# Attention scores: full-width weights of a head pair, 16 KB store runs, and an earlier start of the second unit's transposes

## Chip, cores and metric

One core of a Trainium2 chip. The metric is the device time of an execution in microseconds. PE is the profile's name for TensorE; an eviction is the copy of a finished tile of scores from PSUM into the store tile. Ratios are computed as the mean time of one kernel's fast runs over that of the other's of the same rounds, so a ratio is not quite the ratio of the medians quoted beside it.

## The reference

```python
batch, heads, seq, dim = 8, 8, 512, 64          # q and k, float32
def reference(q, k):
    scale = 1.0 / np.sqrt(q.shape[-1])
    return (np.einsum('bhqd,bhkd->bhqk', q, k) * scale).astype(np.float32)
```

Two inputs of 8.4 MB go in and 67.1 MB of scores come out.

## The kernel before

The work is cut into 4 units of two batches (16 heads, in 8 pairs). Inputs of a unit are loaded, cast to bf16 on GpSimd, and transposed on TensorE. Queries go into a zero-padded tile `qz`, so that one matmul over 128 rows serves the two heads of a pair. `take(ahead, n)` puts `n` steps of the next unit's transposes behind an eviction. A store tile has 32 KB per partition; three such buffers serve loads and stores together.

```python
RO = 16                                     # output rows per run
U = S // RO                                 # 32 runs per head
out_r = out.rearrange("(v b) (t h) (u i) k -> v (b t) (h u) (i k)", b=2, h=4, i=RO)
big_pool = ctx.enter_context(tc.tile_pool(name="big", bufs=3))
...
def matmul(v, t, i, x, dst):
    kT, qz = ts[v]
    pinned(nc.tensor.matmul(out=dst, lhsT=qz[:, i, 2 * t + x, :],        # 64 columns
                            rhs=kT[:, 2 * t + x].rearrange("d m s j -> d (m s j)"),
                            start=True, stop=True))

def scores(v, t):
    o = big_pool.tile([P, RO, S], f32, name="big")
    for i in range(0, RO, 2):
        ps = psum_pool.tile([P, 2, S], f32, name="ps")
        for w in range(2):
            for x in range(2):
                matmul(v, t, i + w, x, ps[half(x), w, :])
        evacuate(o[:, i:i + 2, :], ps)      # ScalarE and VectorE share these
        yield
    src = o.rearrange("p i k -> p (i k)")
    nc.sync.dma_start(out=out_r[v, t], in_=src)
...
for v in range(UNITS):
    ahead = transpose(v + 1, *cast[v + 1]) if v + 1 < UNITS else iter(())
    for t in range(TILES):
        for n, _ in enumerate(scores(v, t)):
            take(ahead, 1 + (n % 4 == 3) if v else 2 * (t > 0))
```

Of the kernel before, what the change touches and what calls it, by code (L numbers as in the profile page):

```python
# [1 line left out]

# [5 lines left out]


@with_exitstack  # L10
def kernel(
    ctx: ExitStack,
    tc: tile.TileContext,
    q: bass.AP,
    k: bass.AP,
    out: bass.AP,
):






    nc = tc.nc
    B, H, S, D = q.shape
    scale = 1.0 / (D ** 0.5)
    P = 128
    UNITS = B // 2
    N = H
    M = P // (2 * H)  # L30
    R = S // M
    J = R // 2
    RO = 16
    U = S // RO
    JJ = J // RO
    IW = 8 // JJ
    TILES = N // 2

    f32 = mybir.dt.float32
    bf16 = mybir.dt.bfloat16  # L40

    q_r = q.rearrange("(v b) g (m j) d -> v (b g m) (j d)", b=2, j=R)
    k_r = k.rearrange("(v b) g (m j) d -> v (b g m) (j d)", b=2, j=R)
    out_r = out.rearrange("(v b) (t h) (u i) k -> v (b t) (h u) (i k)", b=2, h=4, i=RO)

    consts = ctx.enter_context(tc.tile_pool(name="consts", bufs=1))

    big_pool = ctx.enter_context(tc.tile_pool(name="big", bufs=3))
    bf_pool = ctx.enter_context(tc.tile_pool(name="bf", bufs=6))
    t_pool = ctx.enter_context(tc.tile_pool(name="t", bufs=2))  # L50
    tpsum_pool = ctx.enter_context(tc.tile_pool(name="tpsum", bufs=2, space=bass.MemoryType.PSUM))
    psum_pool = ctx.enter_context(tc.tile_pool(name="psum", bufs=3, space=bass.MemoryType.PSUM))


    pinned = tc.keep_in_program_order

    n_evac = 0
    n_tp = 0

    def evacuate(dst, src):  # L60
        nonlocal n_evac

        if n_evac % 6 in (0, 2, 3):
            pinned(nc.scalar.mul(out=dst, in_=src, mul=scale))  # L64
        else:
            pinned(nc.vector.tensor_scalar(out=dst, in0=src, scalar1=scale, scalar2=None,  # L66
                                           op0=mybir.AluOpType.mult))
        n_evac += 1

    def half(h):  # L70
        return slice(h * D, (h + 1) * D)

    def load_and_cast(v):

        xf = big_pool.tile([P, 2, 2, J * D], f32, name="big")
        both = []
        for x, src in enumerate((k_r, q_r)):
            nc.sync.dma_start(out=xf[:, x], in_=src[v].rearrange("p (s c) -> p s c", s=2))
        for x in range(2):
            xb = bf_pool.tile([P, J, 2, D], bf16, name="xb")  # L80
            for s in range(2):
                pinned(nc.gpsimd.tensor_copy(out=xb[:, :, s, :],  # L82
                                             in_=xf[:, x, s].rearrange("p (j d) -> p j d", j=J)))
            both.append(xb)
        return both

    def rearrange(tp, pattern, dst):

        nonlocal n_tp
        copy = (nc.vector.tensor_copy, nc.scalar.copy)[n_tp % 2]  # L90
        n_tp += 1
        for s in range(2):
            src = tp[half(s)].rearrange(pattern, n=N, h=2)
            for h in range(2):
                pinned(copy(out=dst(s, h), in_=src[:, h]))  # L95
                yield

    def transpose(v, kb, qb):


        kT = t_pool.tile([P, N, M, 2, J], bf16, name="kT")
        qz = qzs[v % 2]
        ts[v] = (kT, qz)
        for j0 in range(0, J, 8):
            tp = tpsum_pool.tile([P, 8, P], bf16, name="tp")
            for j in range(8):
                pinned(nc.tensor.transpose(out=tp[:, j, :], identity=identity,  # L107
                                           in_=kb[:, j0 + j].rearrange("p s d -> p (s d)")))
            yield
            yield from rearrange(tp, "d j (n h m) -> d h n m j",  # L110
                                 lambda s, h: kT[half(h), :, :, s, j0:j0 + 8])
        for i0 in range(0, RO, IW):
            tp = tpsum_pool.tile([P, IW, JJ, P], bf16, name="tp")
            for i in range(IW):
                for jj in range(JJ):
                    pinned(nc.tensor.transpose(out=tp[:, i, jj, :], identity=identity,  # L116
                                               in_=qb[:, RO * jj + i0 + i].rearrange("p s d -> p (s d)")))
            yield
            yield from rearrange(tp, "d i jj (n h m) -> d h i n m jj",
                                 lambda s, h: qz[half(h), i0:i0 + IW, :, h * U:(h + 1) * U]  # L120
                                 .rearrange("d i n (m s jj) -> d s i n m jj", s=2, jj=JJ)[:, s])

    def matmul(v, t, i, x, dst):

        kT, qz = ts[v]
        pinned(nc.tensor.matmul(out=dst, lhsT=qz[:, i, 2 * t + x, :],  # L126
                                rhs=kT[:, 2 * t + x].rearrange("d m s j -> d (m s j)"),
                                start=True, stop=True))

    def scores(v, t):  # L130

        o = big_pool.tile([P, RO, S], f32, name="big")
        for i in range(0, RO, 2):
            ps = psum_pool.tile([P, 2, S], f32, name="ps")
            for w in range(2):
                for x in range(2):
                    matmul(v, t, i + w, x, ps[half(x), w, :])
            evacuate(o[:, i:i + 2, :], ps)
            yield
        src = o.rearrange("p i k -> p (i k)")  # L140
        nc.sync.dma_start(out=out_r[v, t], in_=src)  # L141

    def take(steps, count):
        for _ in range(count):
            next(steps, None)

    identity = consts.tile([P, P], dtype=bf16)
    make_identity(nc, identity)
    qzs = [consts.tile([P, RO, N, 2 * U], bf16, name=f"qz{n}") for n in range(2)]
    for qz in qzs:  # L150
        nc.vector.memset(qz, 0.0)  # L151
    cast = [load_and_cast(v) for v in range(UNITS)]

    ts = {}
    for _ in transpose(0, *cast[0]):
        pass
    for v in range(UNITS):
        ahead = transpose(v + 1, *cast[v + 1]) if v + 1 < UNITS else iter(())
        for t in range(TILES):

            for n, _ in enumerate(scores(v, t)):
                take(ahead, 1 + (n % 4 == 3) if v else 2 * (t > 0))
        for _ in ahead:
            pass


# [1 line left out]
_INS = ['q', 'k']  # L168
_OUTS = [((8, 8, 512, 512), 'float32')]


# [23 lines left out]
```

## Time and profile before

| | before |
|---|---|
| median of 4 runs | 203.72 us (203.69 to 203.80) |
| span of the profiled run | 202.1 us |
| score matmuls and weight loads | 512 + 512, weights of 64 columns |
| store packets | 2048 of 32 KB |
| instructions recorded | 1976 |

The lines that bound the kernel are shown in the prediction. Three more from the page: the score matmuls (busy time, mean ns of one, idle time before them), the queue that fetches instructions (packets, MB, share), and the time from a store's issue to its landing.

```profile
L126 PE MATMUL ps<-kT,qz 128*64 128x512 bf16 x512 | 85.0, 456 | 47.2 <-ACT big L64 36.6
...
q8 instruction: 6, 0.10, 0.2%
...
out_dram<-big SPq DMA_DIRECT2D x16, 4096.0 KB, 21.2
```

### The profile page before, as it was taken

Reading aid. Unit: us, or ns where it says so; the run is one execution under the profiler, and the core shown is the slowest. Engines: PE = TensorE matmul, PEld = TensorE weight load, DVE = VectorE, ACT = ScalarE, POOL = GpSimd, SP = SyncE. Lnnn points to the kernel's source line nnn. Section 1 sums busy time; section 2 is a strip of 40 time slices with the busy share of each in tenths; the row PEclk is TensorE's granted clock in tenths of the full one; section 3 lists DMA queues with packets and bytes.
Section 4 is the critical chain, followed back from the end, with each engine's and each line's share of the span. In section 5 each row is a group of like instructions: output and inputs, shape, how many; then the busy total and the mean of one; then the engine's idle time right before and its main releaser. Section 6 shows DMA issues by size and latency. Waiting matters only on the chain.

```text
span 202.1 us, 1976 instructions
## 1 busy us (share of the span) xinstructions
PE 107.7 (53%) x768; PEld 55.7 (28%) x768; DVE 126.4 (63%) x130; ACT 101.1 (50%) x129; POOL 30.5 (15%) x22
## 2 busy tenths in 40 slices
PE   0033488663784767765858685856765366710000
PEld 0033344332342333332423332322322133400000
DVE  6736677974987689997569797479457064530000
ACT  2016665793639586974857566746526241520000
POOL 1277777655000000000000000000000000000000
PEclk9999999998769999997878888888589957555555
DMA  6999999999999999999999999999999999999991
GB/s 214 428 444 415 435 441 422 418 412 428 454 438 417 441 417 428 438 448 435 422 415 425 448 435 448 415 418 428 435 448 441 415 428 438 441 428 441 415 415 58
DMA packets 3464, 84.00 MB, mean 416 GB/s; under 512 B 384, under 2 KB 384, under 8 KB 384
## 3 DMA queue, kind: packets, MB, share of 16 engines
q1 hardware_dynamic: 3456, 83.89, 97.2%
q8 instruction: 6, 0.10, 0.2%
q14 instruction: 2, 0.02, 0.0%
HBM read 16.78 MB, written 67.11 MB: 415 GB/s over the span
## 4 chain that ended last, share of the span: by engine, by line
DMA 33%; DVE 14%; PE 6%; ACT 2%; issue 1%; DVEq 0%; ACTq 0%; SPq 0%
DMA out_dram<-big 33%; DVE big L66 9%; PE ps L126 6%; DVE kT L95 3%; ACT big L64 2%; DVE qz L95 1%; ACT kT L95 1%; PE tp L107 0%; DVEq L66 0%; ACTq L64 0%; SPq L141 0%
## 5 line engine op out<-in xcount | busy, mean ns | idle before, releaser
L126 PE MATMUL ps<-kT,qz 128*64 128x512 bf16 x512 | 85.0, 456 | 47.2 <-ACT big L64 36.6
L66 DVE TENSOR_SCALAR big<-ps 128x1024 f32<-128x1024 f32 x64 | 76.2, 1221 | 38.9 <-DMA out_dram<-big 25.0
L64 ACT ACTIVATE big<-ps 128x1024 f32<-128x1024 f32 x64 | 63.9, 1023 | 56.9 <-DMA out_dram<-big 24.5
L126 PEld LDWEIGHTS <-qz 128*64 128x64 bf16 x512 | 35.6, 124 | 85.9 <-issue 75.7
L82 POOL CAST xb<-big 128x2048 bf16<-128x2048 f32 x16 | 29.8, 1893 | 17.1 <-DMA big<-in_k_dram 9.6
L95 DVE COPY kT<-tp 64x512 bf16<-64x512 bf16 x32 | 22.0, 687 | 7.3 <-PE tp L107 6.9
L95 ACT COPY kT<-tp 64x512 bf16<-64x512 bf16 x32 | 18.5, 578 | 15.2 <-PE tp L107 14.9
L95 DVE COPY qz<-tp 64x512 bf16<-64x512 bf16 x32 | 22.0, 688 | 3.9 <-PE tp L116 3.3
L95 ACT COPY qz<-tp 64x512 bf16<-64x512 bf16 x32 | 18.5, 578 | 4.0 <-PE tp L116 3.6
L107 PE MATMUL tp<-identity,xb 128*128 128x128 bf16 x128 | 12.0, 253 | 15.0 <-POOL xb L82 12.4
L116 PE MATMUL tp<-identity,xb 128*128 128x128 bf16 x128 | 13.3, 272 | 7.8 <-ACT qz L95 4.1
L107 PEld LDWEIGHTS <-xb 128*128 128x128 bf16 x128 | 9.5, 114 | 20.8 <-POOL xb L82 12.4
L116 PEld LDWEIGHTS <-xb 128*128 128x128 bf16 x128 | 10.6, 123 | 14.4 <-issue 14.1
L151 DVE MEMSET qz<- 128x4096 uint32 x2 | 6.9, 3472 | 2.5 <-PEq L179 1.7
L95 ACT ACT_TABLE_LOAD x1 | 1.3, 1283 | 0.7 <-PEq L179 0.7
masks.py:199 POOL TENSOR_SCALAR_AFFINE_SELECT identity<-identity 128x128 bf16<-128x128 bf16 x1 | 0.3, 292 | 0.1
masks.py:197 POOL MEMSET identity<- 128x128 bf16 x1 | 0.2, 204 | 0.3 <-POOLq L179 0.3
L179 POOL MEMSET const-float32-0.0<- 128x1 f32 x1 | 0.1, 98 | 0.2 <-issue 0.2
L179 POOL MEMSET const-bfloat16-1.0<- 128x1 bf16 x1 | 0.1, 101 | 0.0
L179 POOL MEMSET const-uint8-127<- 128x1 uint8 x1 | 0.1, 101 | 0.0
L179 POOL MEMSET const-float32-1.0<- 128x1 f32 x1 | 0.1, 98 | 0.0
## 6 DMA issues: line engine op xcount, KB each, us to landing
out_dram<-big SPq DMA_DIRECT2D x16, 4096.0 KB, 21.2
big<-in_k_dram SPq DMA_DIRECT2D x4, 2048.0 KB, 18.9
big<-in_q_dram SPq DMA_DIRECT2D x4, 2048.0 KB, 23.9
```

Of the source, the lines that this page charges most:

```text
L64: pinned(nc.scalar.mul(out=dst, in_=src, mul=scale))
L66: pinned(nc.vector.tensor_scalar(out=dst, in0=src, scalar1=scale, scalar2=None, op0=mybir.AluOpType.mult))
L82: pinned(nc.gpsimd.tensor_copy(out=xb[:, :, s, :], in_=xf[:, x, s].rearrange("p (j d) -> p j d", j=J)))
L95: pinned(copy(out=dst(s, h), in_=src[:, h]))
L107: pinned(nc.tensor.transpose(out=tp[:, j, :], identity=identity, in_=kb[:, j0 + j].rearrange("p s d -> p (s d)")))
L116: pinned(nc.tensor.transpose(out=tp[:, i, jj, :], identity=identity, in_=qb[:, RO * jj + i0 + i].rearrange("p s d -> p (s d)")))
L126: pinned(nc.tensor.matmul(out=dst, lhsT=qz[:, i, 2 * t + x, :], rhs=kT[:, 2 * t + x].rearrange("d m s j -> d (m s j)"), start=True, stop=T ...
L151: nc.vector.memset(qz, 0.0)
L179: nc = _bacc.Bacc("TRN2", target_bir_lowering=False, num_devices=1)
```

## The change

The intent: weights of the full 128 columns, so that half as many matmuls and weight loads do the same work. For that a partition holds 8 output rows (16 KB) of each of two pairs instead of 16 rows (32 KB) of one. The second unit's transposes begin already with the first store tile.

```diff
-    RO = 16
+    RO = 8
-    out_r = out.rearrange("(v b) (t h) (u i) k -> v (b t) (h u) (i k)", b=2, h=4, i=RO)
+    out_r = out.rearrange("(v b) (t x h) (u i) k -> v (b t) (h u) x (i k)", b=2, x=2, h=2, i=RO)
 ...
-        o = big_pool.tile([P, RO, S], f32, name="big")
-        for i in range(0, RO, 2):
-            ps = psum_pool.tile([P, 2, S], f32, name="ps")
-            for w in range(2):
-                for x in range(2):
-                    matmul(v, t, i + w, x, ps[half(x), w, :])
-            evacuate(o[:, i:i + 2, :], ps)
-            yield
-        src = o.rearrange("p i k -> p (i k)")
-        nc.sync.dma_start(out=out_r[v, t], in_=src)
+        o = big_pool.tile([P, 2, RO, S], f32, name="big")
+        for x in range(2):
+            n = 2 * t + x
+            for i in range(0, RO, 2):
+                ps = psum_pool.tile([P, 2, S], f32, name="ps")
+                for w in range(2):
+                    pinned(nc.tensor.matmul(out=ps[:, w, :], lhsT=qz[:, i + w, n, :],
+                                            rhs=kT[:, n].rearrange("d m s j -> d (m s j)"),
+                                            start=True, stop=True))
+                evacuate(o[:, x, i:i + 2, :], ps)
+                yield
+        nc.sync.dma_start(out=out_r[v, t], in_=o.rearrange("p x i k -> p x (i k)"))
 ...
-    qzs = [consts.tile([P, RO, N, 2 * U], bf16, name=f"qz{n}") for n in range(2)]
+    qzs = [consts.tile([P, RO, N, P], bf16, name=f"qz{n}") for n in range(2)]
 ...
-                take(ahead, 1 + (n % 4 == 3) if v else 2 * (t > 0))
+                take(ahead, 1 + (t > 0 if v == 0 else n % 4 == 3))
```

More of the change, by code (lines that the diff above doesn't have):

```diff
@@ L121, in transpose, with scores @@
                                  .rearrange("d i n (m s jj) -> d s i n m jj", s=2, jj=JJ)[:, s])
-    def matmul(v, t, i, x, dst):
+    def scores(v, t):
         kT, qz = ts[v]
-        pinned(nc.tensor.matmul(out=dst, lhsT=qz[:, i, 2 * t + x, :],
-                                rhs=kT[:, 2 * t + x].rearrange("d m s j -> d (m s j)"),
-                                start=True, stop=True))
-    def scores(v, t):
-        o = big_pool.tile([P, RO, S], f32, name="big")
-        for i in range(0, RO, 2):
-            ps = psum_pool.tile([P, 2, S], f32, name="ps")
-            for w in range(2):
-                for x in range(2):
-                    matmul(v, t, i + w, x, ps[half(x), w, :])
-            evacuate(o[:, i:i + 2, :], ps)
-            yield
-        src = o.rearrange("p i k -> p (i k)")
-        nc.sync.dma_start(out=out_r[v, t], in_=src)
+        o = big_pool.tile([P, 2, RO, S], f32, name="big")
[10 more added lines that the diff above has]
+        nc.sync.dma_start(out=out_r[v, t], in_=o.rearrange("p x i k -> p x (i k)"))
     def take(steps, count):
```

## The prediction

> **What bounds the kernel now.** I read the page from the top. No compute engine is near its limit; the DMA row of the slices is.
>
> ```profile
> span 202.1 us, 1976 instructions
> PE 107.7 (53%) x768; PEld 55.7 (28%) x768; DVE 126.4 (63%) x130; ACT 101.1 (50%) x129; POOL 30.5 (15%) x22
> DMA  6999999999999999999999999999999999999991
> DMA packets 3464, 84.00 MB, mean 416 GB/s; under 512 B 384, under 2 KB 384, under 8 KB 384
> q1 hardware_dynamic: 3456, 83.89, 97.2%
> ```
>
> The busiest compute engine, VectorE, works 63% of the span; the 16 DMA engines work 97.2% of it with one queue's packets, 196.4 us of 202.1 each. Then the stretches, to see where the missing 3% lies and at what rate each phase runs (columns: stretch, its length, the engines' busy times, clock, DMA share, GB/s):
>
> ```profile
> 2.00:4.00 2.00, 0.00 (x0) 0.00 (x0) 2.00 (x1) 0.01 (x1) 0.00 (x0) 1.00 0.73 238
> 5.00:38.00 33.00, 15.42 (x126) 10.51 (x128) 22.10 (x26) 14.31 (x22) 22.38 (x12) 1.00 1.01 430
> 45.00:195.00 150.00, 86.94 (x596) 42.27 (x595) 94.75 (x97) 78.58 (x98) 3.22 (x2) 0.80 1.00 432
> 197.00:199.00 2.00, 0.00 (x0) 0.00 (x0) 0.00 (x0) 0.00 (x0) 0.00 (x0) 0.50 0.31 131
> 199.00:201.00 2.00, 0.00 (x0) 0.00 (x0) 0.00 (x0) 0.00 (x0) 0.00 (x0) 0.50 0.04 16
> ```
>
> From 4 us to 195 us the transfers never pause: loads (5 to 38 us) at 430 GB/s, stores (45 to 195 us) at 432. What is not transfer is about 2 us of start and, at the end, some 6 us in which engines run out one after the other (share 0.31, then 0.04: one straggler) and the program closes. Last, the chain of waits, to see how much room the compute side has inside this:
>
> ```profile
> 120.15 22.27 DMA out_dram<-big
> ...
> 142.52 1.03 ACT big L64
> 143.55 0.04 issue
> 143.60 4.49 PE ps L126 x20
> 148.09 0.02 issue
> 148.11 1.24 DVE big L66
> ...
> 149.40 22.66 DMA out_dram<-big
> ```
>
> A 4 MB store waits for a free 32 KB-per-partition buffer, is filled in 149.40 - 142.42 = 7.0 us, and then takes 22.66 us to land. Its own bytes need 4.194 MB / 432 GB/s = 9.7 us; the other 13 us are queueing behind earlier stores and the landing itself. So the chain alternates fill and store, but the DMA is never empty meanwhile: with three buffers, when one lands, two stores are still due, about 19.4 us of transfer less some 2 us already moved, 17 us against a fill of 7 to 11 us (the store issues in the sync engine's timeline lie 7.4 to 12.9 us apart). The compute side has 6 us or more to spare per tile. **The bound is bytes over DMA rate, plus a cost per packet.**
>
> [...]in its DMA records a 4-byte completion packet takes 9 ns, a 16 KB packet (all 1024 of the loads) 611 ns at the median, a 32 KB packet (all 2048 of the stores) 1213 ns. Two of 611 make 1222, so again 9 ns for one packet more. [...]Before, a store's 32 runs of a head lie side by side and the four heads 1 MiB apart, at 432 GB/s; after, runs are 16 KB apart, with 1 MiB between heads and 2 MiB between the pairs. No run of before shows the new mix; the loads, with rows 16 KB apart, ran at 430. [...]The trace has weight-load gaps of 0.41 to 0.81 us around the transposes[...].
>
> **The change part by part.**
> *Weights.* 512 matmuls with 64 columns become 256 with 128, each still streaming 512 columns; 512 weight loads become 256. In the trace four half-width matmuls that serve one eviction span 0.62 us at full clock, and twenty span 4.49 us at the low clock (0.90 us per eviction): the halves already ran side by side. Two full-width ones should span the same 0.45 to 0.9 us. So half the PE instructions go, and little PE time. On the path that sets the end: 0. The other queue fetches instructions, six packets of 16 KB in the records; were they all for the 768 + 768 PE instructions, each would take 64 bytes (an estimate), and 512 fewer would save two fetches, about 0.6 us each on the DMA engine that serves them, which counts only if that is the straggler. Expected value, an estimate: -0.2 us.
> *Evictions.* 64 + 64 of 128x1024 elements as before, 1.22 us on VectorE and 1.02 on ScalarE. 0.
> *Transposes and copies.* As many tiles (8 per unit) and copies (32 of 512 elements). The destination's inner run of the query copies grows from 2 to 4 elements; copies with runs of 8 (kT) and of 2 (qz) take 687 and 688 ns, so run length is free. 0.
> *Store runs.* Every 32 KB store packet becomes two of 16 KB: 16 stores x 256 = 4096 instead of 2048. By the records 4096 x 611 - 2048 x 1213 = 18,400 ns, over 16 engines 1.15 us each. This lies on the bound, since the engines have no pause in which to hide it: +1.15 us. Nothing else about a store changes: 4 MB, 16 of them, three buffers.
> *Order in the first unit.* The second unit's transposes start with the first store tile: 8 steps there, 16 in the second and third, none in the fourth (before: 0, 16, 16, 8). They need the second unit's casts:
>
> ```profile
> 23.28 3.73 POOL L82 CAST xb<-big 128x2048 bf16<-128x2048 f32 x2 [1.17 <-DMA big<-in_q_dram]
> 28.91 1.23 DVE L66 TENSOR_SCALAR big<-ps 128x1024 f32<-128x1024 f32 x1
> 33.07 3.73 POOL L82 CAST xb<-big 128x2048 bf16<-128x2048 f32 x2 [1.17 <-DMA big<-in_q_dram]
> 35.05 22.20 SPq L141 DMA_DIRECT2D out_dram<-big  x3
> ```
>
> The second unit is cast at 27.0 us, before the first eviction at 28.9, so TensorE will not block. The 8 steps put four copies of 0.69 us on VectorE and two of 0.58 on ScalarE among the evictions: the first store issues at about 36.5 to 37.5 us instead of 35.05. The loads keep the DMA busy until 16.78 MB / 430 GB/s + 2.3 = 41.3 us, so 4 us remain. The second tile can't be filled before the third unit's casts end at 36.8 us, which is so before and after; it has until 51, and issued at 44.06. The third issued at 56.91, waiting for the last casts, and has until 60.7. The fourth comes some 2 us earlier. On the path: 0.
> Sum: 203.74 + 1.15 - 0.2 = 204.7 us. I shade it to 204.6, because the many half-size packets may even out the last microseconds a little.
>
> **The rivals.**
> *The larger strides slow the HBM writes.* [...]Against: [...]the loads ran at the same rate. If the rate lost 3%, stores of 155 us would add 4.7 us: 208.4.
> *The first store comes too late.* For: VectorE gets 2.75 us more work before it, and TensorE takes the transposes in order. Against: the 4 us of slack. If it were missed by 2 us, the DMA would idle 2 us: 206.7.
> *Less PE work makes it faster.* For: TensorE waits and weight loads stand in the chain (PE 6%). Against: a tile filled sooner only joins the queue sooner. Only the straggler could give time: the last engine ends at 200.8 us, the next at 198.9 in the records, so at most 1.9 us of gain, less the 1.15: about 203.
> *Packets stay 32 KB*, read as one run from SBUF: then nothing changes, 203.6.
>
> **Range and chances.** The packet term is worked from three medians that agree, so I trust it to a few tenths if packets do halve. The straggler may move by a microsecond either way without the change being its cause; the runs of before spread only 0.1 us. That gives 203.4 to 205.8. Two per cent is 4.1 us: faster by that would need more than the whole start and end tail that could be won, and I give it 1%. Slower by that needs the stride rival, 2%.
>
> **What would show it.** Right: 4096 store packets (5504 in the hardware queue), 16 KB medians near 611 ns, DMA share 1.0 from 4 to 195 us, store rate 430 instead of 432, 256 matmuls of full width with PE idle more, first store issued near 37 us, and the end about 1 us later. Wrong: a share below 0.97 in any stretch between 36 and 62 us (the order's cost), packets well over 611 ns (strides), or packets still of 32 KB. A straggler that ends much earlier or later than 200.8 us would make the size wrong with the mechanism right.

Passages that nothing in this case shows are cut from this text, and the cuts are marked: a rate that the transfers were compared with (that nothing was left to win inside them was not shown); a reason for a cost per packet, which the records then measure ("in its DMA records" means the trace's); a cause of the weight-load gaps; and reasons for and against the rival of the strides, which stands without a "For". 203.74 + 1.15 - 0.2 = 204.69, told as 204.7 and shaded to 204.6.

## The result

The changed kernel takes 203.02 us (202.95 to 203.29, 4 runs) against 203.72; the ratio is 0.9968, with a 95% interval of 0.995 to 0.9985. It became 0.3% faster where 0.4% slower was forecast, and it lies below the range, which began at 203.4.

The page of the changed kernel: its span, the engines, the DMA row, the packets, and the two queues.

```profile
span 201.3 us, 1456 instructions
PE 99.2 (49%) x503; PEld 48.3 (24%) x512; DVE 126.4 (63%) x130; ACT 100.7 (50%) x129; POOL 30.6 (15%) x22
DMA  6999999999999999999999999999999999999993
DMA packets 5510, 83.97 MB, mean 417 GB/s; under 512 B 384, under 2 KB 384, under 8 KB 384
q1 hardware_dynamic: 5504, 83.89, 98.1%
q8 instruction: 4, 0.07, 0.1%
L132 PE MATMUL ps<-kT,qz 128*128 128x512 bf16 x247 | 81.1, 450 | 55.1 <-ACT big L64 39.2
```

The store packets halved in size as foreseen (5504 in the hardware queue), TensorE's score matmuls are busy almost as long with half the instructions (81.1 us against 85.0), and the DMA row is just as full. The DMA's share rose from 97.2 to 98.1%: its engines do more work in a shorter span, so the gain lies in how the work ends. The stretches show it (the same columns as in the prediction):

```profile
5.00:38.00 33.00, 13.87 (x107) 10.14 (x109) 21.93 (x26) 15.37 (x24) 22.41 (x12) 1.00 1.01 430
45.00:195.00 150.00, 80.85 (x369) 35.95 (x374) 94.31 (x97) 77.73 (x97) 3.74 (x2) 0.80 1.01 430
...
197.00:199.00 2.00, 0.00 (x0) 0.00 (x0) 0.00 (x0) 0.00 (x0) 0.00 (x0) 0.50 0.50 213
199.00:201.00 2.00, 0.00 (x0) 0.00 (x0) 0.00 (x0) 0.00 (x0) 0.00 (x0) 0.50 0.04 16
```

Stores run at 430 GB/s instead of 432, as the prediction said. But from 197 to 199 us half of the engines' time is busy instead of 0.31: more engines end together, later than before, and the last one ends sooner.

The trace makes this exact. It has 16 completion signals for each transfer (384 for the 24 of either kernel), with their times, and at 60, 100, 150 and 190 us its packet records show 16 data packets in flight. I read the 16 signals as one from each of the 16 DMA engines; the trace doesn't say which engine is which. For each store, take the time of the median engine and how far behind it the last one is (all in us, from the profiled run):

| store | before: median | last behind | after: median | last behind |
|---|---|---|---|---|
| 1st | 52.31 | 1.70 | 52.14 | 2.51 |
| 6th | 100.92 | 1.60 | 100.79 | 2.44 |
| 8th | 120.38 | 2.11 | 120.34 | 2.38 |
| 10th | 139.85 | 2.56 | 139.78 | 2.34 |
| 12th | 159.23 | 2.93 | 159.29 | 2.29 |
| 14th | 178.60 | 3.29 | 178.76 | 2.22 |
| 16th | 197.95 | 3.28 | 198.40 | 2.03 |

The median engine ends 0.45 us later, the last one 197.95 + 3.28 - 198.40 - 2.03 = 0.80 us earlier, as the span does (202.1 to 201.3). Before, one engine fell behind steadily, from the 6th store on some 0.2 us per store, until the compute ended at 179 us; after that its lag stood still. The column of the changed kernel needs care: it falls, because it shows whichever engine is last. In that profile one engine was late from the start (2.51 us) and came closer, while the second-last fell behind, from 0.80 us at the 1st store to 2.21 at the 14th; at the end the two are 0.08 us apart. In the run called old order below, which has the same score instructions and packets, the last lag grows from 1.29 us at the 7th store to 2.17 at the 14th and ends at 2.00. So the lag at the first store varies from profile to profile (1.25 to 2.51 us), and the lag at the end repeats (2.03 and 2.00). In the packet records of before, the falling behind shows as one train of 32 KB packets that take mostly 1226 to 1293 ns instead of 1213, each beginning where the one before it ended, from 41.9 to 179 us; their excess sums to 3.9 us. (It is more than the growth in the table, since until the 5th store another engine seems to have been last, whose lag fell.) So there are two questions: does the lag come from the number of PE instructions, from the packet size, or from the order; and what do the packets themselves cost?

### The profile page after: what moved, and what is told of

Same layout as the page of the kernel before. It is cut to its first block, busy times and chain, and to the rows that moved or that the text cites. A ratio compares the mean times of both kernels' runs of the same rounds, so it can differ in the third digit from the quotient of the medians.

```text
span 201.3 us, 1456 instructions
## 1 busy us (share of the span) xinstructions
PE 99.2 (49%) x503; PEld 48.3 (24%) x512; DVE 126.4 (63%) x130; ACT 100.7 (50%) x129; POOL 30.6 (15%) x22
## 3 DMA queue, kind: packets, MB, share of 16 engines
q1 hardware_dynamic: 5504, 83.89, 98.1%
## 4 chain that ended last, share of the span: by engine, by line
DMA 63%; DVE 16%; PE 3%; POOL 3%; ACT 1%; POOLq 1%; issue 1%; SPq 0%; DVEq 0%; ACTq 0%
DMA out_dram<-big 43%; DMA big<-in_q_dram 20%; DVE big L66 12%; PE ps L132 3%; DVE qz L95 3%; POOL xb L82 3%; DVE kT L95 1%; ACT big L64 1%; POOLq L186 1%; SPq L78 0%; DVEq L66 0%; SPq L137 0%; ACTq L64 0%; POOLq L82 0%
## 5 line engine op out<-in xcount | busy, mean ns | idle before, releaser
L132 PE MATMUL ps<-kT,qz 128*128 128x512 bf16 x247 | 81.1, 450 | 55.1 <-ACT big L64 39.2
L132 PEld LDWEIGHTS <-qz 128*128 128x128 bf16 x256 | 27.5, 111 | 96.0 <-issue 83.2
L107 PE MATMUL tp<-identity,xb 128*128 128x128 bf16 x128 | 12.0, 254 | 16.5 <-POOL xb L82 12.5
L116 PE MATMUL tp<-identity,xb 128*128 128x128 bf16 x128 | 12.8, 265 | 6.0 <-DVE kT L95 3.5
L107 PEld LDWEIGHTS <-xb 128*128 128x128 bf16 x128 | 10.5, 116 | 20.8 <-POOL xb L82 12.8
L116 PEld LDWEIGHTS <-xb 128*128 128x128 bf16 x128 | 11.3, 122 | 10.9 <-issue 8.9
```

The costliest lines, as they stand in the source:

```text
L107: pinned(nc.tensor.transpose(out=tp[:, j, :], identity=identity, in_=kb[:, j0 + j].rearrange("p s d -> p (s d)")))
L116: pinned(nc.tensor.transpose(out=tp[:, i, jj, :], identity=identity, in_=qb[:, RO * jj + i0 + i].rearrange("p s d -> p (s d)")))
L132: pinned(nc.tensor.matmul(out=ps[:, w, :], lhsT=qz[:, i + w, n, :], rhs=kT[:, n].rearrange("d m s j -> d (m s j)"), start=True, stop=True))
```

## The experiments

Theory 1: each instruction, on whatever engine, costs one DMA engine a little, and that engine sets the end. Theory 2: smaller packets share the engines out more evenly. Theory 3: the new order of the first unit changes, by chance, how late the last engine is. The first three runs take the change apart.

**Split weights.** The changed kernel with 512 half-width matmuls again.

```diff
-    pinned(nc.tensor.matmul(out=ps[:, w, :], lhsT=qz[:, i + w, n, :], ...))
+    for c in range(2):
+        pinned(nc.tensor.matmul(out=ps[half(c), w, :], lhsT=qz[:, i + w, n, half(c)], ...))
```

> After, with each full-width matmul split again into two column halves: 16 KB runs and the new order, but 512 score matmuls and weight loads as before. Theory 1 (the straggling DMA engine lags in proportion to the PE instructions, by 3.3 us before and 2.0 after): the lag returns, 203.9 to 204.4 us, and the last engine lands some 3 us after the median one. Theory 2 (the finer packets shrink the lag): stays at 203.0. Theory 3 (the order of the first unit): stays at 203.0.

Measured: correct, 204.05 us against 203.81, ratio 1.0007 (0.9994 to 1.0021). The last landing is 2.88 us behind the median. The gain of the change is gone, though packets and order are the new ones: as theory 1 expects, and against the other two.

**Full weights with 32 KB runs.** The kernel before with 256 full-width matmuls.

```diff
-    for x in range(2):
-        matmul(v, t, i + w, x, ps[half(x), w, :])
+    pinned(nc.tensor.matmul(out=ps[:, w, :],
+                            lhsT=ts[v][1][:, i + w, 2 * t:2 * t + 2, :].rearrange("d n c -> d (n c)"),
+                            rhs=ts[v][0][:, 2 * t].rearrange("d m s j -> d (m s j)"), ...))
```

> Before, with 256 full-width score matmuls in place of 512 half-width ones (wrong result on purpose: the lower half of each tile multiplies queries with another pair's keys; the work and the 32 KB runs are the same). Theory 1: gains more than the change did, since it does not pay for the packets: 202.2 to 202.6 us. Theory 2 or 3: as before, 203.6 to 203.8.

Measured: 202.73 us, ratio 0.9945 (0.9933 to 0.9957); the output is wrong. The page and the last stretches of it:

```profile
span 200.9 us, 1455 instructions
...
q1 hardware_dynamic: 3456, 83.89, 97.6%
q8 instruction: 4, 0.07, 0.1%
```

```profile
45.00:195.00 150.00, 81.13 (x372) 36.82 (x377) 94.74 (x97) 78.58 (x98) 3.14 (x2) 0.80 1.00 432
197.00:199.00 2.00, 0.00 (x0) 0.00 (x0) 0.00 (x0) 0.00 (x0) 0.00 (x0) 0.50 0.23 98
199.00:201.00 2.00, 0.00 (x0) 0.00 (x0) 0.00 (x0) 0.00 (x0) 0.00 (x0) 0.50 0.00 0
```

With the packets of before and the instructions of after, the store rate is that of before (432) and no packet starts after 199 us. Theory 1 expected 202.2 to 202.6; the time lies just above that. The two runs and the two kernels make a table of two by two:

| | 512 + 512 PE instructions | 256 + 256 |
|---|---|---|
| 32 KB runs | before: 1 | 0.9945 |
| 16 KB runs | 1.0007 | after: 0.9968 |

Half of the score instructions are worth 0.55% at 32 KB (1.1 us) and 0.39% at 16 KB (0.8 us). Half-size packets cost 0.07% (0.1 us) and 0.23% (0.5 us). The intervals are about 0.15% to each side. The difference along a row (the instructions) is clearly larger; that down a column (the packets) is about as large, so the packets' cost is known only roughly, as 0.1 to 0.5 us, and at 512 + 512 instructions the interval includes 0.

**Old order.** The changed kernel with the `take` line of before.

> After, with the first unit's order of before (second unit transposed from the second tile on). Theory 3: back to 203.7 us. Theories 1 and 2: as after, 203.0 within 0.2.

Measured: correct, 203.10 us, ratio 0.9967 (0.9955 to 0.998). The order does nothing, as the prediction said and for its reason: in the changed kernel the first store issued at 38.23 us, 3.2 us later than before (36.5 to 37.5 was predicted; with the old order it is 35.84), and the DMA still had no pause (share 1.00 to 1.01 from 36 to 62 us). Theory 3 falls.

**Instructions of another engine.** Does it have to be TensorE? GpSimd is idle after the casts, from 48.8 us on in the changed kernel. The changed kernel with 512 tiny memsets there, of which nothing depends on any:

```diff
+    scratch = consts.tile([P, 1], f32, name="scratch")
...
     evacuate(o[:, x, i:i + 2, :], ps)
+    for _ in range(4):
+        pinned(nc.gpsimd.memset(scratch, 0.0))
```

> After, with 512 one-element-wide memsets added on the otherwise idle GpSimd (they run in a burst after the casts, some 50 us). If the lag follows instructions of any engine: 203.5 us or more and a lag above 2.5 us. If it follows PE's instructions alone, or the packets: 203.0.

Measured: correct, 204.68 us, ratio 1.0042 (1.0029 to 1.0055), which is 0.74% or 1.5 us above the changed kernel. The timeline of GpSimd in this run (start, length), and the other instruction queue of the page:

```profile
47.43 79.82 POOL L137 MEMSET scratch<- 128x1 f32 x512
```

```profile
q14 instruction: 6, 0.05, 0.1%
```

The memsets run from 47 to 127 us. The lag of the last engine in the same run: 1.23 us at the 2nd store (61.8 us), 2.79 at the 6th (100.6), 3.84 at the 9th (129.9), 3.94 at the 10th (139.7), then 3.87 at the 12th and 3.66 at the 16th. It grows as long as the memsets run, and stops when they stop. The fetches of instructions don't explain it: this burst added four 8 KB packets of 309 ns each to the instruction queue (6 for 2), at most 1.2 us even if all had hit the same engine, while the lag ends 1.6 us above that of the changed kernel. The times of the fetches settle it. In this run the lag grows by 0.45 us from the 4th store to the 5th (81.2 to 90.9 us), with no fetch recorded between; in the kernel before it grows by 0.30 and 0.31 us at the 8th and 9th store without a fetch (110.7 to 130.1 us), and by 0.14 at the 10th, with one of 928 ns.

**The dose.** Three more kernels differ in the count of `range(4)` alone: 8, 6 and 2 memsets per eviction.

> After with 1024 small GpSimd memsets instead of the 512 of the run before. If each instruction costs the straggling DMA engine a fixed slice (512 cost 1.6 us): another 1.6 us, 206.1 to 206.5 us, and the lag of the last engine near 5 to 5.5 us, growing for as long as the burst lasts (about 160 us at the same pace). If the first 512 only moved a hit onto an engine that was late anyway: 204.5 to 205.

Measured: correct, 210.24 us, ratio 1.0324. The last landing lags 5.53 us, as expected, but the time missed, by a mistake of mine: the burst outlived the stores.

```profile
48.77 160.38 POOL L137 MEMSET scratch<- 128x1 f32 x1024
```

It ends at 209.15 us; the last landing is at 204.0. The time of this run says nothing, its lag does. So the dose was repeated at sizes that end in time.

> After with 768 small GpSimd memsets. The run with 1024 was spoiled by its own burst, which ended after the stores (its last landing lagged by 5.5 us as expected, but its time was set by the memsets); 768 end near 168 us. If the lag grows in proportion to the instructions: last lag 4.3 to 5.0 us (3.66 with 512, 5.53 with 1024), time 205.3 to 205.9 us.

Measured: correct, 205.60 us, ratio 1.0087 (1.0074 to 1.0101), lag 4.36 us. It was run on another chip.

> After with 256 small GpSimd memsets, the lowest dose: lag 2.3 to 3.0 us, time 203.5 to 204.1 us if in proportion. If there is a threshold below which instructions are free: 203.0.

Measured: correct, 203.89 us, ratio 1.0002 (0.9989 to 1.0015), lag 2.87 us. It was run on another chip. Together:

| kernel | memsets | median engine's last landing | last behind | sum | time |
|---|---|---|---|---|---|
| after | 0 | 198.40 | 2.03 | 200.43 | 203.02 |
| | 256 | 198.63 | 2.87 | 201.50 | 203.89 |
| | 512 | 198.64 | 3.66 | 202.30 | 204.68 |
| | 768 | 198.50 | 4.36 | 202.86 | 205.60 |
| | 1024 | 198.47 | 5.53 | 204.00 | (spoiled) |
| before | 0 | 197.95 | 3.28 | 201.23 | 203.72 |
| split weights | 0 | 198.73 | 2.88 | 201.61 | 204.05 |
| full weights, 32 KB | 0 | 197.60 | 2.53 | 200.13 | 202.73 |

The lag is nearly in proportion, 3.0 to 3.4 us per 1000 memsets above the 2.03 us without any, with no threshold down to 256; each lag is from one profile. The median engine hardly moves. The sum belongs to the profiled execution, the time is the median of all; against the profiled execution's own time (203.86 us in before, 203.03 in after, 204.91 with 512 memsets) the rest after the sum is 2.60 to 2.63 us in every row that isn't spoiled. The last engine of the last store sets the end.

**Runs of 8 KB.** To size the packet term apart from the rest, the changed kernel stores 8 KB runs; bytes, result and instructions are the same.

```diff
-    o = big_pool.tile([P, 2, RO, S], f32, name="big")
+    o = big_pool.tile([P, 2, 2, RO // 2, S], f32, name="big")
-    evacuate(o[:, x, i:i + 2, :], ps)
+    evacuate(o[:, i // 4, x, i % 4:i % 4 + 2, :], ps)
-    nc.sync.dma_start(out=out_r[v, t], in_=o.rearrange("p x i k -> p x (i k)"))
+    nc.sync.dma_start(out=out_r[v, t].rearrange("p x (a i) -> p a x i", a=2),
+                      in_=o.rearrange("p a x i k -> p a x (i k)"))
```

> After with store runs of 8 KB (the tile is laid out so that the two pairs alternate; same bytes, same result, same instructions). By the prediction's own term, 9 ns for each packet more: 4096 packets more over 16 engines, +2.3 us, 205.3 us. By what the landings showed between 32 and 16 KB (0.8 us later for the median engine with 2048 packets more, 0.4 to 0.5 us less lag): median engine 1.6 us later, lag 0 to 1 us smaller, 203.6 to 204.6 us.

Measured: correct, 205.00 us, ratio 1.0056 (1.0043 to 1.0068); the range from the landings (203.6 to 204.6) missed, and the prediction's own 9 ns came close.

```profile
45.00:195.00 150.00, 85.53 (x371) 36.97 (x375) 95.06 (x98) 78.70 (x97) 2.90 (x2) 0.78 1.01 422
...
201.00:203.00 2.00, 0.00 (x0) 0.00 (x0) 0.00 (x0) 0.00 (x0) 0.00 (x0) 0.50 0.09 37
```

The rate falls to 422 GB/s. The median engine ends 3.1 us later (201.50), and only 0.75 us ahead of the last. A packet takes 312 ns at the median, so nearly 7 ns more than half of 611. But the cost is not one constant: the first four stores of this run land 9.77 us apart, and from about 90 us on 10.0, while the lag falls from 1.7 to 0.7, with jumps up of 0.4 and 0.9 us at the 7th and 12th store, just before which a fetch of 879 ns is recorded: here a fetch seems to have hit the last engine. In stretches that no instruction fetch disturbs, stores of 32 KB packets land 9.67 to 9.68 us apart and those of 16 KB packets 9.71 to 9.72, which is 5 ns for each packet more (40 ns for the 8 packets more per store that an engine has in the mean). I have no run that explains the later pace of the 8 KB stores.

**Relieving an engine.** An attempt to take work off the late engine at the end: the last store in three pieces.

```diff
+    if (v, t) == (UNITS - 1, TILES - 1):
+        nc.sync.dma_start(out=out_r[v, t][:, 0], in_=of[:, 0])
+        nc.sync.dma_start(out=out_r[v, t][0:120, 1], in_=of[0:120, 1])
+        nc.sync.dma_start(out=out_r[v, t][120:128, 1], in_=of[120:128, 1])
```

> After with the last store in three: the first pair on all 16 DMA engines, the second pair's first 120 partitions and its last 8 apart. If the 120 go to 15 engines, one engine is relieved of 8 packets (4.9 us). If that is the one that collects the lag with each instruction, the last landing of the second piece lags by under 1.5 us and the time falls by up to 0.5 us; if it is another one, the lag stays at 2 us, some engines get one packet more, and the time is 203.0 to 203.8.

Measured: correct, 206.74 us, ratio 1.0138 (1.0125 to 1.0151), outside both expectations. The trace has 15 data completions for the piece of 120 partitions, which by the reading above are 15 engines (the hardware queue has 5527 packets instead of 5504, as 16, 15 and 8 completions in place of 16 make it). But that piece is slow:

```profile
185.00:190.00 5.00, 0.00 (x0) 0.00 (x0) 0.00 (x0) 0.00 (x0) 0.00 (x0) 0.50 1.02 436
190.00:195.00 5.00, 0.00 (x0) 0.00 (x0) 0.00 (x0) 0.00 (x0) 0.00 (x0) 0.50 1.01 367
195.00:200.00 5.00, 0.00 (x0) 0.00 (x0) 0.00 (x0) 0.00 (x0) 0.00 (x0) 0.50 0.90 239
```

The engines are 90% busy at 239 GB/s: each packet takes longer (1049 ns at the median of the 16 KB packets that began from 195 to 200 us, 613 from 185 to 190). Whether the 120 partitions or the 8 beside them do that was not separated. Which engine is the late one stays unknown, and none of these runs gave a correct kernel better than the changed one.

## Why the prediction was wrong

- **What bounds the kernel: right.** The DMA has no pause, and compute had room; 430 GB/s and 5504 packets came as written.
- **Weights, "On the path that sets the end: 0" and "-0.2 us": this step failed.** Leaving out half of the score instructions was worth 0.8 to 1.1 us. The prediction read the DMA as 16 equal engines, with a mean of 196.4 us of work each, and asked of every part what it adds to the mean. The end was set by the one engine that was late, and its lag grew with the number of instructions executed while it stored: 2.03 us after, 2.88 with split weights, 3.66 with 512 memsets. The records of before had shown the straggler, and the rival "Less PE work makes it faster" even named "about 203". It was set aside: I allowed only the two fetches, at 0.6 us each (recorded are 0.89 to 1.03 us for those of before), and put the rest down to chance ("The straggler may move by a microsecond either way without the change being its cause").
- **Store runs, "+1.15 us": the mechanism right, the size too large; this term failed too.** Measured between kernels of equal instructions, 0.1 to 0.5 us. Two reasons show in the trace. Packets of one engine overlap (by 3 to 4 ns mostly in the train of before), so that their durations must not be added: the landings give 5 ns per packet instead of 9, 128 x 5 = 0.64 us. And the last engine loses less than the median one: with the smaller packets its lag fell by 0.40 us (3.28 to 2.88) and 0.50 us (2.53 to 2.03). After the compute has ended, the lag stands still with 32 KB packets (3.29, 3.31, 3.28) and falls with 16 KB packets (2.22, 2.11, 2.03). Why is not shown.
- **Order, evictions, copies: right,** no run shows a cost of them. The rivals of the strides and of the late first store did not come true: 430 GB/s and no pause. The weight-load gaps of 0.41 to 0.81 us before the transposes mostly went, to 0.28 us or none; what caused them is not shown.
- **The sum:** the change is -1.1 us for the instructions (at 32 KB) and +0.5 for the packets, where -0.2 and +1.15 were forecast. (That the two add up to the measured -0.7 within rounding proves nothing: the second is the rest after the first.) Of the miss of 1.6 us, the instructions make 0.9 and the packets 0.7.
- **Open:** what an instruction does to that DMA engine, and whether it is the same engine in every run. Recorded fetches don't come when it happens. Every timed run here lists the core's span and clock, so each was recorded in some form; whether an execution without recording has the lag is not known.

## What to carry to other kernels

In this kernel, bound by DMA, the end belonged to the last engine of the last transfer: the time less its landing was 2.60 to 2.63 us in every profiled execution of the table that isn't spoiled. In another such kernel, look at each engine's completions over time, and not only at the mean share. If one falls behind while compute runs and stops when compute stops, then instructions far off the critical path may have a price. Here, in executions that were all recorded, it was some 1.6 to 3 ns each: 0.8 to 1.1 us for 512 on TensorE (256 matmuls and 256 weight loads), 1.5 us for 512 on GpSimd. A change that only removes instructions can win that much, as long as no other engine is then the last. Take packet costs from the spacing of transfers, not from the sum of packet durations: here they gave 5 and 9 ns per packet.
